# Five small edits to a hybrid attention and feed-forward block: the bias line by GpSimd copies, one transpose for the index weights, the values bank by bank, a split copy, and the last norm on VectorE

## The chip, the core and the metric

The program runs on one core of a Trainium2 chip. A core has a matrix engine (TensorE, PE in the profile, with its weight load PEld), VectorE (DVE), ScalarE (ACT), GpSimd (POOL) and SyncE (SP), which here issues most of the loads. The five run their own instruction streams and wait for each other on semaphores. DMAs are issued from SP, ScalarE or GpSimd. The metric is the device time of one execution in microseconds, the median over several runs; lower is better.

## The reference, cut to what matters

One layer on x of 512 frames by 1024 channels. All projections come from one matrix; branch A is sparse attention with an indexer that picks 128 keys for a query and a relative bias, branch B is stick-breaking attention. A gated MLP follows.

```python
q_a, k_a, v_a, q_i, k_i, w_i, q_s, k_s, v_s, g_a, g_b = split(x @ w_in)
w_i = w_i * 8 ** -0.5
# branch A, for a block of 128 queries
dots = einsum('thd,sd->ths', q_i, k_i) * 64 ** -0.5
score = einsum('th,ths->ts', w_i, relu(dots))      # chunk-causal
sel = top_k(score, 128)
logits = q_a @ k_a[sel] * 64 ** -0.5 + rel_bias[t5_bucket(sel - t)]
y_a = softmax(logits) @ v_a[sel]
# branch B
a = exp(log_sigmoid(z) + sum over later keys of log_sigmoid(-z));  y_s = a @ v_s
x = layer_norm(alpha * x + (sigmoid(g_a) * (y_a @ W_a) + sigmoid(g_b) * (y_s @ W_s)) @ w_out)
u, g = split(x @ w_ffn_in)
x = layer_norm(alpha * x + (gelu(causal_dwconv(u)) * g) @ w_ffn_out)
```

The bias depends on the distance alone. `t5_bucket` gives one of 32 buckets: distances 0 to 7 one each, then eight wider ones (from 8, 12, 16, 23, 32, 46, 64 and 91 on), and the same again for keys behind the query.

## The kernel before, in words

Every 32-bit operand of a matmul is split in a high part (rounded to the matrix engine's format) and the rest, so a product is three matmuls: high by high, high by low, low by high. For a weight piece, `Stream._advance` issues the load into one of three raw buffers (SP), the high copy on ScalarE (`whi_...`, L105) and the subtraction on VectorE or GpSimd (`wlo_...`, L107). A raw buffer can be loaded again once the subtraction has read it, so a piece three ahead is issued when that is done.

The program goes from stage to stage. Nine matmuls on zeros (`WARM`, into `idle_ps`) run while the first loads are on their way. Then come the indexer's queries (`qi0` to `qi7`, four PSUM banks `qi_ps`, 384 columns: the first 128 queries need no selection), the indexer's keys with the index weights (`ki`, 72 rows), and then a list of pieces, `FILL`: branch B's values `vs`, queries and keys `qs`, `ks`, the gates `gb`, branch A's `qa`, `ka`, `va`, with the heads of both branches worked in between. Values are made by `proj_v`: four weight pieces of two chunks each, four PSUM banks of one row block each, from the pool `psA` of four banks; `vs_ps` takes over the banks of `qi_ps`, so its matmuls into the fourth bank wait until the last indexer query (`qi3a`, `qi3b`, from `idx_queries`) has been read. When all is summed, ScalarE copies a bank's high part into `va`, VectorE writes the rest (L336, L337). `gb_ps` is the next user of the banks of `va_ps`.

The bias line holds, for each of 8 heads, the bias of all 640 distances. In before it is a product of a one-hot matrix (64x640, loaded by GpSimd in two halves) with the table's high and low parts (`rb`), in two matmuls (`line_ps`, L270), which ScalarE copies out negated (L271). GpSimd then stores it (`s_line`), and writes `s_win`, 128 shifted copies for every head, in DRAM. A head of branch A later loads its window `win` from there by SP (L483).

The index weights come out of the `ki` product as 8 rows and are needed as columns: three transposes of 8x128 into `wi_ps` (L367).

The order of all instructions is set by a scheduler with a timeline model, not written by hand, so an edit can move instructions in other places. The last part is the feed-forward product's last rows and the norm of the last row block (`finish(3)`), whose output goes out in three pieces.

Of the kernel before, what the change touches and what calls it, by code (L numbers as in the profile page):

```python
# [11 lines left out]
F32 = mybir.dt.float32  # L12
# [5 lines left out]
S = 512  # L18
D = 1024
DFF = 2816  # L20
H = 8
# [6 lines left out]
EPS = 1e-5  # L28
HT = 256
NSEL = 128  # L30
BIG = 1.0e30
INVALID = -3.0e38
TAKEN = -3.3e38
# [16 lines left out]
def r32(ap):  # L50
    return ap.bitcast(F32)


class Stream:


    def __init__(self, nc, raw, ring, pieces, ahead_load, ahead_split, place=None, lo_on_pool=()):
        self.nc, self.raw, self.ring, self.pieces = nc, raw, ring, pieces
        self.place = {} if place is None else place
        self.lo_on_pool = set(lo_on_pool)  # L60
        self.al, self.asp = ahead_load, ahead_split
        self.loaded, self.split, self.used = {}, {}, 0
        self.mixed, self.homes, self.direct, self.before = {}, {}, set(), {}
        self.nl = self.ns = 0

    def _advance(self, upto):
# [24 lines left out]
        while self.ns < min(n, upto + self.asp, self.nl):  # L91
            ts, w = self.loaded.pop(self.ns)
            key = self.pieces[self.ns][0]
            if key in self.direct:
                self.split[self.ns] = ts
                self.ns += 1
                continue
            if key in self.mixed:
                parts = self.mixed[key](ts)
            else:  # L100
                parts = [(ts[0], w, key)]
            out = ()
            for t, w, where in parts:
                hi, lo = self.tiles(where)
                nc.scalar.activation(hi[:, :w], t[:, :w], AF.Copy)  # L105
                eng = nc.gpsimd if key in self.lo_on_pool else nc.vector
                self.low = eng.tensor_sub(lo[:, :w], t[:, :w], r32(hi[:, :w])).ins  # L107
                out += (hi, lo)
            self.split[self.ns] = out
            self.ns += 1  # L110
# [20 lines left out]
def tile_block(ctx: ExitStack, tc: tile.TileContext, xT, xN, w_qi, w_ki, w_t, w_v, w_br, w_o, w_fi, w_fo,  # L131
# [10 lines left out]
    def padded(pool, shape, dt=F32, **kw):  # L142

        n = int(np.prod(shape[1:]))
        t = pool.tile([shape[0], -(-n // 32) * 32], dt, **kw)[:, :n]
        return t if len(shape) == 2 else t.rearrange("p (a b) -> p a b", a=shape[1])
# [84 lines left out]
    def load_x(key):  # L231
        k = int(key[2:])
        xraw[k] = bp.tile([128, 512], F32, tag="k", bufs=4, name=f"xr{k}")
        nc.sync.dma_start(xraw[k], xT[k * 128:(k + 1) * 128, :])

    for k in range(KC):
        st.before[f"qi{k}"] = load_x
    for k in range(KC):
# [15 lines left out]
    nc.gpsimd.dma_start(cwt.rearrange("p a b -> p (a b)"), cw)  # L254


    ohf = bp.tile([64, NREL], F32, tag="beta", bufs=2, name="ohf")
    oh = bp.tile([64, NREL], F32R, tag="beta", bufs=2, name="oh")
    rb = edge.tile([64, H], F32R, name="rb")
    rbf = padded(bp, [32, H], name="rbf")  # L260
    for r in (slice(0, 32), slice(32, 64)):
        nc.gpsimd.dma_start(ohf[r], onehot)
    nc.gpsimd.dma_start(rbf, rel)
    nc.gpsimd.tensor_copy(oh, ohf)
    nc.vector.tensor_copy(rb[0:32], rbf)
    nc.vector.tensor_sub(rb[32:64], rbf, r32(rb[0:32]))
    line = bp.tile([H, NREL], F32, tag="beta", bufs=2, name="line")
    for a, b in ((0, 512), (512, NREL)):
        ps = pb("line_ps")
        nc.tensor.matmul(ps[:H, :b - a], rb, oh[:, a:b], start=True, stop=True)  # L270
        nc.scalar.activation(line[:, a:b], ps[:H, :b - a], AF.Copy, scale=-1.0)  # L271
    s_line = nc.dram_tensor("s_line", (H, NREL), F32, kind="Internal").ap()
    s_win = nc.dram_tensor("s_win", (H, 128, 512), F32, kind="Internal").ap()
    nc.gpsimd.dma_start(s_line, line)
# [43 lines left out]
    def proj_v(which, name):  # L318

        pss = [pa(f"{name}_ps{i}") for i in range(NB)]  # L320
        for g in range(4):
            wh, wl = st.get(f"{which}{g}")
            for kk in range(2):
                k = 2 * g + kk
                c = slice(kk * 512, kk * 512 + 512)
                for i in range(NB):
                    r = slice(i * 128, i * 128 + 128)
                    nc.tensor.matmul(pss[i], xh[k][:, r], wh[:, c], start=(k == 0), stop=False)
                    nc.tensor.matmul(pss[i], xh[k][:, r], wl[:, c], start=False, stop=False)
                    nc.tensor.matmul(pss[i], xl[k][:, r], wh[:, c], start=False, stop=(k == KC - 1))  # L330
                    yield 3
        vt = []
        for i in range(NB):
            v = bp.tile([128, H, 2, 64], F32R, tag="v", bufs=4, name=f"{name}{i}")
            src = pss[i].rearrange("p (h d) -> p h d", h=H)
            nc.scalar.activation(v[:, :, 0, :], src, AF.Copy)  # L336
            nc.vector.tensor_sub(v[:, :, 1, :], src, r32(v[:, :, 0, :]))  # L337
            vt.append(v)
        return vt


# [2 lines left out]
    def idx_queries():  # L344
        for n in range(4):
# [6 lines left out]
            nc.vector.tensor_sub(b[0:64, late], ps[64:128], r32(b[64:128, late]))  # L352
            qi.extend((a, b))

    def idx_keys():
        ps = whole(proj_t("ki", M=72, bank=pb))
        kih = bp.tile([128, 512], F32R, tag="pt", bufs=8, name="kih")
        kil = bp.tile([128, 512], F32R, tag="pt", bufs=8, name="kil")
        wiT = bp.tile([8, 512], F32, tag="pt", bufs=8, name="wiT")
        nc.scalar.activation(wiT, ps[64:72], AF.Copy, scale=float(H) ** -0.5)  # L360
        for r in (slice(0, 64), slice(64, 128)):
            nc.scalar.activation(kih[r], ps[0:64], AF.Copy)
            nc.vector.tensor_sub(kil[r], ps[0:64], r32(kih[0:64]))
        wi = padded(cst, [128, 3, H], name="wi")
        ps = pb("wi_ps")
        for j in (1, 2, 3):
            nc.tensor.transpose(ps[:, (j - 1) * H:j * H], wiT[:, j * 128:j * 128 + 128], ident[:H, :H])  # L367
        nc.vector.tensor_copy(wi.rearrange("p a b -> p (a b)"), ps[:, :3 * H])
        index["k"] = kih, kil, wi

    score = {j: bp.tile([128, 128 * (j + 1)], F32, name=f"score{j}") for j in (1, 2, 3)}
# [539 lines left out]
    def finish(j):  # L911
        r = x1[j]
        mv, rstd = norm_stats(r, parts2[j])
        if j < 3:
            for c in (slice(0, 512), slice(512, 1024)):
                norm_apply(r, r, mv, rstd, g2, b2, c)
                nc.scalar.dma_start(out[j * 128:(j + 1) * 128, c], r[:, c])
            return
        cs = (slice(0, SHARE // 2), slice(SHARE // 2, SHARE), slice(SHARE, 1024))
        for c in (slice(512, 1024), slice(0, 512)):  # L920
            nc.vector.scalar_tensor_tensor(r[:, c], r[:, c], mv[:, 0:1], g2[:, c], op0=ALU.subtract, op1=ALU.mult)
        nc.scalar.activation(r[:, cs[2]], r[:, cs[2]], AF.Copy, scale=rstd)
        nc.gpsimd.tensor_add(r[:, cs[2]], r[:, cs[2]], b2[:, cs[2]])
        for c in cs[:2]:
            nc.vector.scalar_tensor_tensor(r[:, c], r[:, c], rstd, b2[:, c], op0=ALU.mult, op1=ALU.add)
        for c in cs:
            nc.scalar.dma_start(out[j * 128:(j + 1) * 128, c], r[:, c])


    for t in range(2):  # L930
# [123 lines left out]
```

## Time and profile before

| | us |
|---|---|
| median of 3 runs | 762.4 (762.27 to 762.73) |
| the profiled execution | 762.05 |
| its span, first to last instruction | 760.2 |
| TensorE busy | 751.1 (99%) |
| VectorE busy | 547.1 (72%) |
| ScalarE busy | 374.1 (49%) |
| GpSimd busy | 119.3 (16%) |
| moved by DMA | 107.09 MB, mean 141 GB/s |

A row of a timeline gives the start, the length, the engine, the line of the kernel, the operation, what it writes and reads, the form, a count of instructions in it, and in brackets the idle time in front of it with what ended it. A row of the waits gives who waited for what, the sum, how often and the longest. A row of the DMA issues gives what is loaded, the queue, the count, KB each, and the median from issue to landing. A matmul's length overlaps the next one's, so the distance between starts is what it costs.

### The profile page before, as it was taken

What the parts mean: (1) busy time and instruction counts of PE and PEld (TensorE: products, weight loads), DVE (VectorE), ACT (ScalarE), POOL (GpSimd) and SP (SyncE); (2) the same over time, 40 slices, a digit from 0 to 9 for tenths busy, and PEclk for the clock granted to TensorE, in tenths of its full rate; (3) what the DMA queues carried; (4) which work ended last, traced back from release to release, by engine and by line L of the source; (5) the groups of instructions that cost most, each with busy time, mean ns of one, the idle gap of its engine ahead of it and who ended that gap; (6) DMA issues with size and microseconds to landing.
All of it is one profiled execution on the core that took longest, in us unless ns stands there. A gap on an engine that the chain in (4) does not pass through costs nothing.

```text
span 760.2 us, 9908 instructions
## 1 busy us (share of the span) xinstructions
PE 751.1 (99%) x3597; PEld 630.3 (83%) x3597; DVE 547.1 (72%) x912; ACT 374.1 (49%) x601; POOL 119.3 (16%) x127
## 2 busy tenths in 40 slices
PE   9999999999999999999999999999999999999996
PEld 7788888888888888888889888888888888888885
DVE  6689587999675454458865778767877786777776
ACT  6554656555686857935311534433443443344320
POOL 3002555425834210000010000000000000000011
PEclk9999999999999999999999999999999999999999
DMA  8643423132333333126801554354434434445971
GB/s 258 225 155 100 123 83 111 57 111 84 111 98 97 102 106 99 55 78 203 328 1 42 166 181 147 117 180 170 135 138 164 169 129 147 168 153 157 340 291 56
DMA packets 38449, 107.09 MB, mean 141 GB/s; under 512 B 4536, under 2 KB 4936, under 8 KB 38400
## 3 DMA queue, kind: packets, MB, share of 16 engines
q1 hardware_dynamic: 34016, 95.73, 37.1%
q10 hardware_dynamic: 2576, 6.29, 3.2%
q0 software_dynamic: 1808, 4.44, 1.8%
q8 instruction: 28, 0.46, 0.2%
q14 instruction: 21, 0.17, 0.1%
HBM read 91.48 MB, written 12.87 MB: 137 GB/s over the span
## 4 chain that ended last, share of the span: by engine, by line
PE 92%; POOL 3%; issue 2%; DVE 2%; ACT 1%; DVEq 0%; POOLq 0%
PE u_ps L741 5%; PE u_ps L740 5%; PE g_ps L741 5%; PE u_ps L739 5%; PE g_ps L740 5%; PE g_ps L739 5%; PE m_ps L829 4%; PE m_ps L831 4%; PE m_ps L830 4%; PE av_ps L436 2%; PE ga_ps L285 2%; PE ga_ps L286 2%; PE ga_ps L287 2%; PE o_ps L698 2%; PE o_ps L699 2%
## 5 line engine op out<-in xcount | busy, mean ns | idle before, releaser
L739 PE MATMUL u_ps<-x1h,whi_u 128*128 128x512 f32 (+1 forms) x192 | 71.4, 372 | 0.0
L741 PE MATMUL u_ps<-x1h,wlo_u 128*128 128x512 f32 (+1 forms) x192 | 71.4, 372 | 0.0
L740 PE MATMUL u_ps<-x1l,whi_u 128*128 128x512 f32 (+1 forms) x192 | 71.3, 371 | 0.0
L739 PE MATMUL g_ps<-x1h,whi_g 128*128 128x512 f32 (+1 forms) x184 | 69.9, 380 | 0.0
L740 PE MATMUL g_ps<-x1l,whi_g 128*128 128x512 f32 (+1 forms) x184 | 69.9, 380 | 0.0
L741 PE MATMUL g_ps<-x1h,wlo_g 128*128 128x512 f32 (+1 forms) x184 | 69.9, 380 | 0.0
L748 POOL MEMSET u<- 128x2 f32 x22 | 2.1, 100 | 250.1 <-DVE c L753 250.1
L740 PEld LDWEIGHTS u_ps<-x1l,whi_u 128*128 128x128 f32 x192 | 36.2, 188 | 6.3
L739 PEld LDWEIGHTS u_ps<-x1h,whi_u 128*128 128x128 f32 x192 | 36.2, 188 | 6.2
L741 PEld LDWEIGHTS u_ps<-x1h,wlo_u 128*128 128x128 f32 x192 | 36.2, 188 | 6.2
L740 PEld LDWEIGHTS g_ps<-x1l,whi_g 128*128 128x128 f32 x184 | 34.6, 188 | 6.6
L739 PEld LDWEIGHTS g_ps<-x1h,whi_g 128*128 128x128 f32 x184 | 34.6, 188 | 6.5
L741 PEld LDWEIGHTS g_ps<-x1h,wlo_g 128*128 128x128 f32 x184 | 34.6, 188 | 6.5
L425 DVE TENSOR_TENSOR ptl<-tr_ps,pth 128x512 fp32r<-128x512 f32 (+1 forms) x48 | 27.4, 595 | 14.0 <-ACT pth L424 13.7
L107 DVE TENSOR_TENSOR wlo_u<-raw,whi_u 128x1024 fp32r<-128x1024 f32 x22 | 26.9, 1221 | 9.8 <-ACT whi_u L105 9.8
L105 ACT ACTIVATE whi_g<-raw 128x1024 fp32r<-128x1024 f32 x22 | 23.3, 1061 | 20.5 <-PE m_ps L831 13.6
L105 ACT ACTIVATE whi_pa<-raw 128x1024 fp32r<-128x1024 f32 x11 | 11.7, 1061 | 40.8 <-PE u_ps L740 32.3
L754 ACT ACTIVATE c<-c,cwt 128x512 f32<-128x512 f32 x22 | 15.8, 716 | 30.0 <-DVE c L753 30.0
L105 ACT ACTIVATE whi_u<-raw 128x1024 fp32r<-128x1024 f32 x22 | 23.3, 1060 | 13.9 <-PE u_ps L740 9.0
L107 DVE TENSOR_TENSOR wlo_g<-raw,whi_g 128x1024 fp32r<-128x1024 f32 x22 | 26.8, 1218 | 3.1 <-ACT whi_g L105 3.1
L488 POOL TENSOR_TENSOR bm<-win,score 128x256 f32<-128x256 f32 (+2 forms) x24 | 26.9, 1148 | 9.0 <-DVE mn L503 8.9
L758 DVE TENSOR_TENSOR hp<-g_ps,c 128x512 f32<-128x512 f32 x22 | 15.2, 691 | 17.3 <-PE g_ps L741 15.8
(559 smaller groups left out, 2205.9 us busy)
## 6 DMA issues: line engine op xcount, KB each, us to landing
raw<-in_w_fi_dram SPq DMA_DIRECT2D x44, 512.0 KB, 3.3
raw<-in_w_t_dram SPq DMA_DIRECT2D x32, 512.0 KB, 3.3
raw<-in_w_fo_dram SPq DMA_DIRECT2D x21, 512.0 KB, 3.5
rawb_p<-in_w_fo_dram SPq DMA_DIRECT2D x11, 512.0 KB, 3.7
d_z<-s_sum SPq DMA_DIRECT2D x10, 512.0 KB, 7.4
raw<-in_w_v_dram SPq DMA_DIRECT2D x8, 512.0 KB, 4.3
raw<-in_w_br_dram SPq DMA_DIRECT2D x8, 512.0 KB, 3.3
raw<-in_w_o_dram SPq DMA_DIRECT2D x8, 512.0 KB, 4.3
```

The costliest lines, as they stand in the source:

```text
L105: nc.scalar.activation(hi[:, :w], t[:, :w], AF.Copy)
L107: self.low = eng.tensor_sub(lo[:, :w], t[:, :w], r32(hi[:, :w])).ins
L285: nc.tensor.matmul(ps[:M], wh[:, c], xh[k], start=(k == 0), stop=False)
L425: lows = nc.vector.tensor_sub(tl[:, :width], ps[:, :width], r32(th[:, :width]))
L488: nc.gpsimd.tensor_add(bm[:, OFF[j]:OFF[j] + N], win[:, 512 - N:512], score[j])
L739: nc.tensor.matmul(ps[:, c], wh[:, kc], x1h[:, k, c], start=(k == 0), stop=False)
L740: nc.tensor.matmul(ps[:, c], wh[:, kc], x1l[:, k, c], start=False, stop=False)
L741: nc.tensor.matmul(ps[:, c], wl[:, kc], x1h[:, k, c], start=False, stop=(k == KC - 1))
L754: nc.scalar.activation(c, c, AF.Gelu_apprx_tanh, bias=cwt[:, f, 3:4])
L829: nc.tensor.matmul(o, xh_[:, r], wh[:, c], start=start, stop=False, skip_group_check=True)
L830: nc.tensor.matmul(o, xh_[:, r], wl[:, c], start=False, stop=False, skip_group_check=True)
L831: mm = nc.tensor.matmul(o, xl_[:, r], wh[:, c], start=False, stop=stop, skip_group_check=True)
```

## The change

Five edits. The bias line is written by GpSimd: the table is loaded turned (`relT`, 8x32), negated, and copied into the line in 18 pieces, one for each run of distances with one bucket. The one-hot matrix, `rb` and both matmuls go. The index weights are copied to rows 0, 32 and 64 of a zeroed 128x128 tile and transposed at once. In `proj_v`, the last of the four pieces is worked bank by bank, both chunks of a bank in a row, and each bank is copied out where its sum ends. The high copy of `qi0` is made in two halves. In the last norm VectorE does all three pieces itself, and the middle one goes out by SP instead of ScalarE.

```diff
+FAR = [8, 12, 16, 23, 32, 46, 64, 91]
...
-                nc.scalar.activation(hi[:, :w], t[:, :w], AF.Copy)
+                cuts = [0, w // 2, w] if key in self.halved else [0, w]
+                for a, b in zip(cuts, cuts[1:]):
+                    nc.scalar.activation(hi[:, a:b], t[:, a:b], AF.Copy)
...
+    st.halved.add("qi0")
...
-    ohf = bp.tile([64, NREL], F32, tag="beta", bufs=2, name="ohf")
-    oh = bp.tile([64, NREL], F32R, tag="beta", bufs=2, name="oh")
-    rb = edge.tile([64, H], F32R, name="rb")
-    rbf = padded(bp, [32, H], name="rbf")
-    for r in (slice(0, 32), slice(32, 64)):
-        nc.gpsimd.dma_start(ohf[r], onehot)
-    nc.gpsimd.dma_start(rbf, rel)
-    nc.gpsimd.tensor_copy(oh, ohf)
-    nc.vector.tensor_copy(rb[0:32], rbf)
-    nc.vector.tensor_sub(rb[32:64], rbf, r32(rb[0:32]))
+    relT = padded(bp, [H, 32], name="relT")
     line = bp.tile([H, NREL], F32, tag="beta", bufs=2, name="line")
-    for a, b in ((0, 512), (512, NREL)):
-        ps = pb("line_ps")
-        nc.tensor.matmul(ps[:H, :b - a], rb, oh[:, a:b], start=True, stop=True)
-        nc.scalar.activation(line[:, a:b], ps[:H, :b - a], AF.Copy, scale=-1.0)
+    nc.gpsimd.dma_start(relT, rel.rearrange("b h -> h b"))
+    nc.gpsimd.tensor_scalar(relT, relT, -1.0, None, op0=ALU.mult)
+    zero = S - 1
+    nc.gpsimd.tensor_copy(line[:, zero - 7:zero + 1], relT[:, 0:8][:, ::-1])
+    nc.gpsimd.tensor_copy(line[:, zero + 1:zero + 8], relT[:, 17:24])
+    for n, (lo_, hi_) in enumerate(zip(FAR, FAR[1:] + [S])):
+        for b, u0, u1 in ((8 + n, zero - hi_ + 1, zero - lo_ + 1), (24 + n, zero + lo_, min(zero + hi_, NREL))):
+            nc.gpsimd.tensor_copy(line[:, u0:u1], relT[:, b:b + 1].to_broadcast([H, u1 - u0]))
...
             wh, wl = st.get(f"{which}{g}")
-            for kk in range(2):
+            steps = [(kk, i) for kk in range(2) for i in range(NB)]
+            if g == 3:
+                steps.sort(key=lambda s_: s_[1])
+            for kk, i in steps:
...
+                if k == KC - 1:
+                    v = bp.tile([128, H, 2, 64], F32R, tag="v", bufs=4, name=f"{name}{i}")
+                    src = pss[i].rearrange("p (h d) -> p h d", h=H)
+                    nc.scalar.activation(v[:, :, 0, :], src, AF.Copy)
+                    nc.vector.tensor_sub(v[:, :, 1, :], src, r32(v[:, :, 0, :]))
+                    vt.append(v)
+                yield 3
...
-        nc.scalar.activation(wiT, ps[64:72], AF.Copy, scale=float(H) ** -0.5)
+        for j in (1, 2, 3):
+            nc.scalar.activation(wiT[32 * j - 32:32 * j - 24], ps[64:72, j * 128:j * 128 + 128], AF.Copy,
+                                 scale=float(H) ** -0.5)
...
-        for j in (1, 2, 3):
-            nc.tensor.transpose(ps[:, (j - 1) * H:j * H], wiT[:, j * 128:j * 128 + 128], ident[:H, :H])
-        nc.vector.tensor_copy(wi.rearrange("p a b -> p (a b)"), ps[:, :3 * H])
+        nc.tensor.transpose(ps[:, :128], wiT, ident)
+        nc.vector.tensor_copy(wi, ps[:, :96].rearrange("p (a b) -> p a b", b=32)[:, :, :H])
...
-        nc.scalar.activation(r[:, cs[2]], r[:, cs[2]], AF.Copy, scale=rstd)
-        nc.gpsimd.tensor_add(r[:, cs[2]], r[:, cs[2]], b2[:, cs[2]])
-        for c in cs[:2]:
+        for c, eng in zip(cs, (nc.scalar, nc.sync, nc.scalar)):
             nc.vector.scalar_tensor_tensor(r[:, c], r[:, c], rstd, b2[:, c], op0=ALU.mult, op1=ALU.add)
-        for c in cs:
-            nc.scalar.dma_start(out[j * 128:(j + 1) * 128, c], r[:, c])
+            eng.dma_start(out[j * 128:(j + 1) * 128, c], r[:, c])
```

What this does to the order of instructions is shown at three places. The rows name the line, the operation, what it writes and reads with the number of the buffer, the shape, and in brackets the semaphores it waits for (Pool, DVE, Activation and PE are engines, DMAHW the loads of SP and ScalarE, DMASW those of GpSimd).

GpSimd before the first head, before:

```order
L262 DMA ohf_323<-in_onehot_dram 32x640 x2
L263 DMA rbf_326<-in_rel_dram 32x8
L455 MEMSET keep_830 128x1
L215 AFFINE_SELECT first_96<-first_96 128x512 [waits Pool_49]
L455 MEMSET keep_931 128x1
L220 MEMSET mhalf_101 128x1 [waits Activation_49]
L264 CAST oh_324<-ohf_323 64x640 [waits DMASW2_49,DMASW3_49,DVE_49,PE_49]
L274 DMA s_line<-line_333 8x640 [waits Activation_49]
L275 DMA s_win<-s_line 1024x1x512 [waits DMASW5_49]
```

and after, from the scaling of the table on (its load stands behind that of cwt):

```order
L265 TENSOR_SCALAR relT_324<-relT_324 8x32 [waits DMASW2_49]
L267 COPY line_325<-relT_324 8x8 [waits Pool_49]
L268 COPY line_325<-relT_324 8x7
L271 COPY line_325<-relT_324 8x4 x4
L271 COPY line_325<-relT_324 8x7 x2
L271 COPY line_325<-relT_324 8x9 x2
L271 COPY line_325<-relT_324 8x14 x2
L271 COPY line_325<-relT_324 8x18 x2
L271 COPY line_325<-relT_324 8x27 x2
L271 COPY line_325<-relT_324 8x421
L271 COPY line_325<-relT_324 8x38
L274 DMA s_line<-line_325 8x640 [waits Pool_49]
```

The copies, which wait for GpSimd itself and the table's load (DMASW2), have taken the place of the CAST, and the store of the line no longer waits for ScalarE.

SP at the values' last pieces (w_v is vs0 to vs3 here, w_t the first piece of the list behind them, qs0), before:

```order
L87 DMA raw_11_0_369<-in_w_v_dram 128x1024 [waits DMAHW3_49,DMAHW0_49,DVE_49]
L87 DMA raw_12_0_418<-in_w_v_dram 128x1024 [waits DMAHW1_49,DVE_49]
L87 DMA raw_13_0_500<-in_w_t_dram 128x1024 [waits DMAHW5_49,DMAHW2_49,DVE_49]
L483 DMA win_1956<-s_win 128x512 [waits DMASW6_49]
L483 DMA win_2089<-s_win 128x512
L87 DMA raw_14_0_602<-in_w_t_dram 128x1024 [waits DMAHW3_49,DVE_49]
```

and after:

```order
L89 DMA raw_11_0_377<-in_w_v_dram 128x1024 [waits DMAHW3_49,DMAHW0_49,DVE_49]
L89 DMA raw_12_0_425<-in_w_v_dram 128x1024 [waits DMAHW1_49,DVE_49]
L488 DMA win_1963<-s_win 128x512 [waits DMAHW5_49,DMASW4_49]
L89 DMA raw_13_0_507<-in_w_t_dram 128x1024 [waits DMAHW2_49,DVE_49]
L488 DMA win_2096<-s_win 128x512
L89 DMA raw_14_0_609<-in_w_t_dram 128x1024 [waits DMAHW3_49,DVE_49]
```

The first of two window loads, which waits for `s_win` (DMASW), now stands ahead of the load of qs0.

TensorE and VectorE at the last piece of `va`. TensorE before (`va_ps0` to `va_ps3` are the four banks, `xh6` and `xh7` the two chunks):

```order
L328 MATMUL va_ps0_1940<-whi_va3_1946,xh6_283 128x512
L329 MATMUL va_ps0_1940<-wlo_va3_1947,xh6_283 128x512 [waits Pool_49]
L330 MATMUL va_ps0_1940<-whi_va3_1946,xl6_284 128x512
L328 MATMUL va_ps1_1941<-whi_va3_1946,xh6_283 128x512
L329 MATMUL va_ps1_1941<-wlo_va3_1947,xh6_283 128x512
L436 MATMUL av_ps_2052<-pth_2011,vs0_731 128x512 [waits DVE_49,Activation_49]
L330 MATMUL va_ps1_1941<-whi_va3_1946,xl6_284 128x512
L328 MATMUL va_ps2_1942<-whi_va3_1946,xh6_283 128x512
L436 MATMUL av_ps_2052<-ptl_2012,vs0_731 128x512 [waits DVE_49]
```

and after:

```order
L331 MATMUL va_ps0_1947<-whi_va3_1953,xh6_284 128x512
L332 MATMUL va_ps0_1947<-wlo_va3_1954,xh6_284 128x512 [waits Pool_49]
L333 MATMUL va_ps0_1947<-whi_va3_1953,xl6_285 128x512
L331 MATMUL va_ps0_1947<-whi_va3_1953,xh7_306 128x512
L332 MATMUL va_ps0_1947<-wlo_va3_1954,xh7_306 128x512
L441 MATMUL av_ps_2059<-pth_2018,vs0_720 128x512 [waits DVE_49,Activation_49]
L333 MATMUL va_ps0_1947<-whi_va3_1953,xl7_307 128x512
L331 MATMUL va_ps1_1948<-whi_va3_1953,xh6_284 128x512
L441 MATMUL av_ps_2059<-ptl_2019,vs0_720 128x512 [waits DVE_49]
```

The second chunk of the first bank (`xh7`, `xl7`) stood 17 rows behind the first one and now follows it at once. VectorE before:

```order
L503 ISA lg_2096,mn_2097<-l_ps_2100,bm_2092 128x512 [waits DMASW3_49,DMASW2_49,DMASW5_49,PE_49,Pool_49]
L503 ISA mn_2097 128x1
L503 ISA lg_2096,mn_2097<-l_ps_2105,win_2089 128x128 [waits PE_49]
L503 ISA mn_2097 128x1
L337 TENSOR_TENSOR va0_2201<-va_ps0_1940,va0_2201 128x8x64 [waits Activation_49]
L337 TENSOR_TENSOR va1_2204<-va_ps1_1941,va1_2204 128x8x64 [waits Activation_49]
```

and after:

```order
L508 ISA lg_2103,mn_2104<-l_ps_2107,bm_2099 128x512 [waits DMASW3_49,PE_49,Pool_49]
L508 ISA mn_2104 128x1
L338 TENSOR_TENSOR va0_2189<-va_ps0_1947,va0_2189 128x8x64 [waits Activation_49]
L508 ISA lg_2103,mn_2104<-l_ps_2112,win_2096 128x128 [waits PE_49]
L508 ISA mn_2104 128x1
L338 TENSOR_TENSOR va1_2199<-va_ps1_1948,va1_2199 128x8x64 [waits Activation_49]
```

The rest of the first bank (`va0`) is now taken ahead of the 128-column logits of branch A's head, and that of the second behind them.

Elsewhere a few matmuls of `qi` change places, and where the trace of before has 40 to 75 us some dots of the indexer move by a few matmuls against those of `vs`, `qs` and `ks`, and the copies of `vs` with them; the rest of the program stands in the same order.

More of the change, by code (lines that the diff above doesn't have):

```diff
@@ L63, in __init__ @@
         self.mixed, self.homes, self.direct, self.before = {}, {}, set(), {}
+        self.halved = set()
         self.nl = self.ns = 0
@@ L320, in proj_v @@
         pss = [pa(f"{name}_ps{i}") for i in range(NB)]
+        vt = []
         for g in range(4):
             wh, wl = st.get(f"{which}{g}")
-            for kk in range(2):
+            steps = [(kk, i) for kk in range(2) for i in range(NB)]
+            if g == 3:
+                steps.sort(key=lambda s_: s_[1])
+            for kk, i in steps:
                 k = 2 * g + kk
                 c = slice(kk * 512, kk * 512 + 512)
[L326 to L338, printed above, removed]
+                r = slice(i * 128, i * 128 + 128)
+                nc.tensor.matmul(pss[i], xh[k][:, r], wh[:, c], start=(k == 0), stop=False)
+                nc.tensor.matmul(pss[i], xh[k][:, r], wl[:, c], start=False, stop=False)
+                nc.tensor.matmul(pss[i], xl[k][:, r], wh[:, c], start=False, stop=(k == KC - 1))
+                if k == KC - 1:
[5 more added lines that the diff above has]
+                yield 3
         return vt
@@ L353, in idx_queries @@
             qi.extend((a, b))
+    wiT = bp.tile([128, 128], F32, name="wiT")
+    nc.gpsimd.memset(wiT, 0.0)
     def idx_keys():
@@ L358, in idx_keys @@
         kil = bp.tile([128, 512], F32R, tag="pt", bufs=8, name="kil")
-        wiT = bp.tile([8, 512], F32, tag="pt", bufs=8, name="wiT")
-        nc.scalar.activation(wiT, ps[64:72], AF.Copy, scale=float(H) ** -0.5)
+        for j in (1, 2, 3):
+            nc.scalar.activation(wiT[32 * j - 32:32 * j - 24], ps[64:72, j * 128:j * 128 + 128], AF.Copy,
+                                 scale=float(H) ** -0.5)
         for r in (slice(0, 64), slice(64, 128)):
```

## The prediction

> **What bounds the kernel now.** I read the busy shares first, then TensorE's waits over the whole run.
>
> ```profile
> PE 751.1 (99%) x3597; PEld 630.3 (83%) x3597; DVE 547.1 (72%) x912; ACT 374.1 (49%) x601; POOL 119.3 (16%) x127
> ...
> PE idle_ps L208 <- DVE idle L205: 1.2, 1, 1.2
> PE gb_ps L285 <- DVE va L337: 0.3, 1, 0.3
> ```
>
> TensorE (PE) is busy for 99% of the 760.2 us span and waits twice in all. An edit on another engine therefore pays only if it takes work off PE, closes that second wait, or shortens what stands after PE's last matmul. It costs only where it makes PE wait anew. The profiled execution took 762.05 us, 1.85 more than its span; the median of the runs is 762.4, so I work out a difference and put it on the median. About 0.2%, 1.5 us, is what a measurement of this kernel can tell from no change.
>
> **The bias line, on PE.** The timeline where its two matmuls stand (start, length):
>
> ```profile
> 15.44 0.86 PE L251 MATMUL qi_ps<-xh,wlo_qi 128*128 128x384 f32 x4
> 16.23 0.45 PE L270 MATMUL line_ps<-oh,rb 64*8 64x512 f32 x2
> 16.90 0.34 PE L250 MATMUL qi_ps<-xl,whi_qi 128*128 128x384 f32 x1
> ```
>
> Four matmuls of 384 columns take 0.86 and one alone 0.34, so they start (0.86 − 0.34)/3 = 0.173 apart. From 15.44 four of them and one more (L249) bring L250 to 16.31; it starts at 16.90. The line's matmuls thus cost 0.59. Without them everything behind could start 0.59 earlier, if what it needs is there.
>
> **Who is late next.** PE's first use of the fourth bank of vs_ps waits for VectorE's last indexer query (qi3b), which frees that bank:
>
> ```profile
> 16.72 8.50 SPq L87 DMA_DIRECT2D raw<-in_w_v_dram  x4
> 22.55 1.06 ACT L105 ACTIVATE whi_vs<-raw 128x1024 fp32r<-128x1024 f32 x1 [3.49 <-DMA raw<-in_w_v_dram]
> 23.64 1.22 DVE L107 TENSOR_TENSOR wlo_vs<-raw,whi_vs 128x1024 fp32r<-128x1024 f32 x1 [3.80 <-ACT whi_vs L105]
> 30.18 0.56 DVE L352 TENSOR_TENSOR qi3b<-qi_ps,qi3b 64x384 fp32r<-64x384 f32 x1
> 30.62 0.62 PE L328 MATMUL vs_ps<-whi_vs,xh 128*128 128x512 f32 x2
> ```
>
> The load of the first values weight (vs0) goes out at 16.72 and releases ScalarE at 22.55. From there VectorE works without a break (wlo_vs, the queries, wlo_vs, qi3a, qi3b) to 30.74. The second matmul of the last row, at 30.85 (0.62 less one matmul's 0.39 behind 30.62), is the one that needs the bank. Its margin is 0.11. If PE comes 0.59 earlier it stands there for about 0.48, since this chain hangs on the load and not on PE. Call d the shift of vs0's landing: the line part ends as d − 0.11, and never below −0.59.
>
> **What moves d.** The line is now written by 18 GpSimd copies behind a load of 256 four-byte numbers. What these stand against (GpSimd's timeline, its groups, and DMA issues with KB and us to landing):
>
> ```profile
> 9.79 0.80 POOL L264 CAST oh<-ohf 64x640 fp32r<-64x640 f32 x1 [4.53 <-DMA ohf<-in_onehot_dram]
> 18.25 0.54 POOL L274 DMA_DIRECT2D s_line<-line  x1 [7.66 <-ACT line L271]
> 23.99 1.13 POOL L275 DMA_DIRECT2D s_win<-s_line  x1 [5.20 <-DMA s_line<-line]
> ...
> L484 POOL MEMSET win<- 64x64 f32 x8 | 1.2, 146 | 54.1 <-DMA win<-s_win 54.1
> ...
> rbf<-in_rel_dram POOLq DMA_DIRECT2D x1, 1.0 KB, 6.0
> s_win<-s_line POOLq DMA_DIRECT2D x1, 2048.0 KB, 17.2
> raw<-in_w_t_dram SPq DMA_DIRECT2D x1, 512.0 KB, 6.9
> ...
> raw<-in_w_t_dram SPq DMA_DIRECT2D x32, 512.0 KB, 3.3
> ```
>
> GpSimd waited 4.53 for ohf, to 9.79. One load of 1 KB, which as rbf took 6.0, takes the place of three issues, so I put its landing near 9. One scaling and 18 copies cost 2.8 if each takes the 0.146 of a 64x64 memset, 15 if each takes the 0.80 of the CAST, and little over 0 if they overlap. I take 2.5, nearest the memset, since all but one copy write 8 rows of 38 numbers or fewer. The line is ready near 11.5 instead of 17.96. GpSimd was waiting in all of this (7.66 in the second row), so the copies hide. s_line and s_win follow as before, 5.74 apart: s_win is issued near 17.3 instead of 23.99, its traffic from about 18.9 on.
>
> [...]
>
> In before, s_win left at 23.99, when vs0 to vs2 had landed or nearly so. Now it meets them. Stretches by PE, PEld, DVE, ACT, POOL busy time, clock, DMA share, GB/s:
>
> ```profile
> 19.00:22.50 3.50, 3.50 (x22) 3.50 (x22) 0.76 (x1) 0.05 (x1) 0.00 (x0) 1.00 0.97 348
> 25.50:34.00 8.50, 8.50 (x38) 6.39 (x37) 7.61 (x11) 5.73 (x9) 0.00 (x0) 1.00 0.79 237
> ```
>
> From 19 to 22.5 the 16 engines are full without s_win. Beside s_win, from 25.5 to 34, all traffic together is 237 GB/s, and a 512 KB load takes 6.9 instead of the 3.3 of such loads later. So the upper end of d is +3.6. The lower end is −0.5: 160 KB of onehot (64x640 numbers of 4 bytes) are gone, at 348 GB/s 0.46 us of transfer ahead of the x and qi loads on which the issue at 16.72 hangs. Near which? vs0 is issued 2.2 before s_win's traffic begins, and at a landing of 3.3 to 5.8 most of its bytes are ahead of it; vs1 and vs2 behind it meet s_win fully, but ScalarE turns to vs1 only at 26.5. I take d = +0.4, nearer the lower end, so the line part is +0.3: the 0.59 that PE gains is lost, and a little more.
>
> The Trainium skill's "DMA: Bandwidth & Descriptors" (section "Issuing engines are not separate DMA queues") says that transfers issued by SP, ScalarE and GpSimd run on the same 16 engines and interleave, which speaks against the earlier s_win. The 6.9 against 3.3 agrees; it is the rule behind the slower rival below.
>
> On SP's queue one of the two win loads now stands ahead of the load of qs0 (raw_13 in the order).
>
> ```profile
> SPq L483 <- DMA s_win<-s_line: 11.2, 1, 11.2
> 41.24 1.06 ACT L105 ACTIVATE whi_qs<-raw 128x1024 fp32r<-128x1024 f32 x1 [1.52 <-PE vs_ps L330]
> ```
>
> That wait of 11.2 now holds qs0's load too. s_win should land near 17.3 + 17.2 = 34.5, plus up to 2 for sharing; the load then takes 3.3 to 6.9, so 38 to 43. ScalarE takes it at 41.24, after 1.52 of waiting for PE. I count 0; up to +1.5 if ScalarE's relus behind it run late and PE's dots with them. The next loads leave earlier than 42.08, since SP is free sooner.
>
> **Index weights.** Three transposes of eight rows become one of 128x128:
>
> ```profile
> 34.24 0.39 PE L329 MATMUL vs_ps<-wlo_vs,xh 128*128 128x512 f32 x1
> 34.56 0.35 PE L367 MATMUL wi_ps<-ident,wiT 8*128 8x8 f32 x3
> 34.84 0.50 PE L330 MATMUL vs_ps<-whi_vs,xl 128*128 128x512 f32 x1
> ...
> 206.49 0.49 PE L420 MATMUL tr_ps<-ident,lg 128*128 128x128 f32 x3
> 206.74 0.48 PE L330 MATMUL va_ps<-whi_va,xl 128*128 128x512 f32 x1
> ```
>
> A 512-column matmul holds PE 0.23 (0.62 less 0.39 above), so L330 could start at 34.47; with the transposes it starts some 0.48 later (its own length of 0.50 instead of 0.39 holds the last 0.11). Three 128x128 transposes take 0.25 at 206.49, 0.08 each. The part saves 0.40; bounds 0.2 and 0.48. ScalarE's three copies instead of one lie where PE waits for nothing, and cost nothing as long as they end before PE reaches 34.47; GpSimd's memset of wiT lies in the wait of 4.53.
>
> **Values' last piece.** ScalarE and VectorE at the wait that PE has left:
>
> ```profile
> 199.90 0.39 PE L330 MATMUL va_ps<-whi_va,xl 128*128 128x512 f32 x1
> 207.53 0.50 PE L285 MATMUL gb_ps<-xh,whi_gb 128*128 128x512 f32 x1 [0.32 <-DVE va L337]
> 202.23 0.37 ACT L424 ACTIVATE pth<-tr_ps 128x256 fp32r<-128x256 f32 x1
> 206.18 1.54 ACT L336 ACTIVATE va<-va_ps 128x512 fp32r<-128x512 f32 x3
> 204.35 0.68 DVE L503 CUSTOM_DVE_ANT_0 lg<-l_ps,bm 128x512 f32<-128x512 f32 x1
> 204.96 0.28 DVE L503 CUSTOM_DVE_ANT_0 lg<-l_ps,win 128x128 f32<-128x128 f32 x1
> 206.79 1.29 DVE L337 TENSOR_TENSOR va<-va_ps,va 128x512 fp32r<-128x512 f32 x2 [1.54 <-ACT va L336]
> 206.06 0.60 PE L499 MATMUL l_ps<-ka0b,qa0b 128*128 128x384 f32 x2
> ```
>
> Behind 206.74 and 0.23 for that matmul, gb_ps could start at 206.97; it starts at 207.53, 0.56 later. In the new order the first bank's last matmul stands where 199.90 stands now, ScalarE empties it behind the pth copy (from 202.6), VectorE right behind its 512-column lg (205.03) until 205.68 (half of 1.29), over 1 us before PE comes. Saved 0.56; bounds 0.32 (the wait as the profile labels it) and 0.56. That eviction now stands ahead of VectorE's 128-column lg, which moves from 205.24 to 205.96; l_ps of 384 columns waits for the bank that it frees, and starts at 206.06 plus two transposes put ahead of it, 206.23: 0.27 of margin. For vs PE waits nowhere in before; the dots around it move by a few rows, which I count at 0.
>
> **First weight's high half.** 0, since PE is in its nine warming matmuls until 5.22 and the half that is cut is done at 4.74; the cut's second start-up on ScalarE, some 0.1, can use the 0.48 up to there.
>
> ```profile
> 1.20 4.02 PE idle_ps L208 x9
> 4.11 0.63 ACT L105 ACTIVATE whi_qi<-raw 128x512 fp32r<-128x512 f32 x1
> ```
>
> **Last norm.**
>
> ```profile
> 752.85 0.41 DVE L907 SCALAR_TENSOR_TENSOR r<-m_end,r 128x256 f32<-128x256 f32 x1
> 755.61 1.61 DVE L925 SCALAR_TENSOR_TENSOR r<-r,rstd,ln 128x384 f32<-128x384 f32 x2
> ```
>
> The two 384s take 1.61 beside GpSimd's add, where 256 columns take 0.41, so that a 384 alone should take 0.62. Three in a row on VectorE are 0.41 + 0.62 + 0.62, to 757.26 instead of 757.22, less some overlap of one with the next. ScalarE issues two outputs instead of three, SP the other. I take −0.1; bounds −0.4 (the 1.61 less two of 0.62) and +0.1.
>
> **Sum.** +0.3 − 0.40 − 0.56 + 0 − 0.1 = −0.76: 761.3 for the profiled execution, 761.6 on the median.
>
> **Rivals.** (1) Nothing is late: onehot's absence brings vs0 0.5 earlier, and PE keeps its 0.59. Sum −0.59 − 0.40 − 0.56 − 0.1 = −1.65, 760.8; with the tail at its best 760.5. For it: s_win may start after vs0's bytes. Against: the full engines from 19 to 22.5. (2) Slower: the earlier s_win takes half of the engines from vs0's last bytes on, d = +3.6. Then +3.5 − 1.06 = +2.4, 764.8. It decides the sign from d = 1.2 on, and makes it measurably slower from d = 2.7 on. (3) The banks do not come free early, because ScalarE or VectorE reaches va later than I lay out: the 0.56 stays, and with d = 0.4 it is 762.2. (4) qs0's load behind the window holds PE by 1 to 1.5 on top of my sum: 762.6 to 763.1.
>
> **How the numbers follow.** Forecast with d between −0.3 and 1.2: 0.45. Rival 1: 0.25. Rival 2 with d over 1.2: 0.14, three fifths of it over 2.7. Rival 3: 0.07. Rival 4: 0.09. Faster by over 0.2% is under 760.9: rival 1's 0.25 and 0.04 of the forecast's lower edge, 0.29. Slower by over 0.2% is over 763.9: 0.08 of rival 2, 0.03 of the fourth with a larger d, and 0.03 for a stall in the reordered stretch from 40 to 75 that no row prices, 0.14. Between them 0.57. The range runs from rival 1 at its best, 760.5, to d = 2.2, 763.4, and leaves out most of rival 2.
>
> **What the profile after would show.** No line_ps on PE. s_win issued at 16 to 19. whi_vs starting within 0 to 1.2 of 22.55, and a new PE wait on VectorE's qi3b near 30 of 0.5 to 1. The wait of gb_ps gone. One transpose for wi_ps. The second win load early on SP and qs0's load behind it near 35. VectorE ending near 757 less the shift. If whi_vs starts by 22.1, rival 1 is right; past 24, rival 2.

## The result and the profile after

The changed kernel takes 772.27 us (median of 4 runs, 771.72 to 772.96), against 762.36 for the kernel before, measured beside it: ratio 1.013, 95% interval 1.0112 to 1.0147. The forecast was 761.6, with a range up to 763.4. The profiled execution took 771.72 us, its span 769.9; before, these were 762.05 and 760.2. So 9.7 us of span were added.

First the busy shares and TensorE's waits of the changed kernel, which answer to the first two views of before:

```profile
PE 761.3 (99%) x3593; PEld 628.8 (82%) x3593; DVE 547.7 (71%) x911; ACT 373.8 (49%) x601; POOL 123.7 (16%) x143
...
PE idle_ps L212 <- DVE idle L209: 1.2, 1, 1.2
```

PE has four instructions fewer, and the wait of `gb_ps` is gone, as it should be. Yet PE is busy for 10.2 us more. It isn't waiting longer; it is working more slowly. The granted clock doesn't explain it: the mean is 0.998 in both executions. The plainest sign is a stretch of 100 us in the feed-forward product, where neither the code nor its order was changed. First before, then after (columns: stretch, busy time of PE, PEld, DVE, ACT and POOL with counts, granted clock, DMA share, GB/s):

```profile
500.00:600.00 100.00, 100.00 (x443) 82.81 (x442) 74.82 (x110) 42.58 (x60) 0.80 (x8) 1.00 0.42 147
```

```profile
500.00:600.00 100.00, 100.00 (x432) 80.55 (x431) 71.45 (x105) 41.22 (x58) 0.70 (x7) 1.00 0.43 151
```

PE is full and at clock 1.00 in both, but has 432 matmuls in the 100 us instead of 443. The timeline shows the step from one to the next, before:

```profile
499.53 0.39 PE L741 MATMUL u_ps<-x1h,wlo_u 128*128 128x512 f32 x1
...
501.12 0.39 PE L739 MATMUL u_ps<-x1h,whi_u 128*128 128x512 f32 x1
```

and after:

```profile
500.09 0.39 PE L745 MATMUL g_ps<-x1l,whi_g 128*128 128x512 f32 x1
...
501.49 0.39 PE L745 MATMUL u_ps<-x1l,whi_u 128*128 128x512 f32 x1
```

There are seven steps between the two rows of before, 1.59/7 = 0.227 us each, and six between those of after, 1.40/6 = 0.233. Each 512-column matmul costs some 0.006 to 0.007 more, without a wait that a profile could list. By the start of the first `u_ps` the changed kernel is 2.76 late (408.79 against 406.03), by the last one 9.11 (691.56 against 682.45).

### The profile page after: what moved, and what is told of

Same layout as the page of the kernel before. It is cut to its first block, busy times and chain, and to the rows that moved or that the text cites. A ratio compares the mean times of both kernels' runs of the same rounds, so it can differ in the third digit from the quotient of the medians.

```text
span 769.9 us, 9907 instructions
## 1 busy us (share of the span) xinstructions
PE 761.3 (99%) x3593; PEld 628.8 (82%) x3593; DVE 547.7 (71%) x911; ACT 373.8 (49%) x601; POOL 123.7 (16%) x143
## 4 chain that ended last, share of the span: by engine, by line
PE 98%; DVE 1%; issue 0%; DVEq 0%
PE g_ps L746 5%; PE u_ps L746 5%; PE g_ps L745 5%; PE u_ps L745 5%; PE u_ps L744 5%; PE g_ps L744 5%; PE m_ps L834 4%; PE m_ps L835 4%; PE m_ps L836 4%; PE av_ps L441 3%; PE tr_ps L425 2%; PE gb_ps L287 2%; PE ga_ps L287 2%; PE ga_ps L286 2%; PE ga_ps L285 2%; PE gb_ps L286 2%
```

## The experiments

What the diff moves without showing it are addresses. A tile is a named buffer in the core's memory, and a pool a stretch of that memory for some tiles; pools are stacked from the left end or from the right one. `rb` (64 partitions of 8 numbers, 32 bytes in each) was the only tile of the small pool `edge`, which lies on the right-hand side of the core's memory, ahead of nearly all other tiles there. Without it, every tile on that side (`xh`, `xl`, `qi`, `r`, `x1h`, `x1l` and the rest) lies 32 bytes further on: `x1h` starts at byte 178880 of a partition before and at 178912 after, by the compiled program. The ring, the pool of the weights' high and low halves (`whi`, `wlo`) on the left, stays: the first `whi` is at 29888 in both. What a padding tile of so many bytes does can be tried without touching one instruction: in the kernels that only pad, every engine's instructions and order are those of the changed kernel. "Distance" below is that of right-hand tiles from the ring, counted from before's, which is 178880 − 29888 = 148992, 582 times 256. In the changed kernel it is +32.

**The 32 bytes given back.** The edit to the changed kernel:

```diff
+    pad = edge.tile([64, 8], F32, name="pad")
```

> The changed kernel with one unused tile of 32 bytes in the pool edge, where rb stood; every instruction stands in the same place as in the changed kernel. Theory A (layout): the removal of rb moved every tile on the right side by 32 bytes, from addresses that are a multiple of 64 to ones that are not, and each 512-column matmul on them takes 0.233 instead of 0.227. With the pad the spacing is 0.227 again and the time is the one that the five edits give alone, 760.0 to 761.6. Theory B (something else in the edits, such as the earlier traffic of s_win or the instruction stream, slows the matmuls): the pad changes nothing, 771.7 to 773.

It took 760.24 us (759.58 to 760.68) against 763.13 for before, measured beside it, ratio 0.9959 (0.9945 to 0.9973), span 758.5. The same stretch of it:

```profile
500.00:600.00 100.00, 100.00 (x443) 82.81 (x442) 76.28 (x112) 43.28 (x60) 0.79 (x8) 1.00 0.43 146
```

The 443 matmuls are back, and with them 11.4 us of span (769.9 to 758.5). This is the fast kernel, below. By the spans of the two traces the five edits themselves gain 1.7 us (760.2 to 758.5), and the shift of the tiles costs 11.4. The 1.7 is less sure than the 11.4: it hangs on one trace of each kernel, and by the medians the gain is 2.9 (760.24 against 763.13).

**The kernel before, pushed 32 bytes the other way.**

```diff
-    rb = edge.tile([64, H], F32R, name="rb")
+    rb = edge.tile([64, 2 * H], F32R, name="rb")[:, :H]
```

> The kernel before with rb 64 bytes wide instead of 32 (half of it unused), nothing else; every instruction stands in the same place. Theory A: all right-side tiles move by 32 bytes off the multiple of 64, the matmuls slow down as in the changed kernel, 771 to 774. Theory B: 762.4, as before.

774.03 us (773.85 to 775.91), ratio 1.0147 (1.0125 to 1.0168).

```profile
500.00:600.00 100.00, 100.00 (x432) 80.73 (x431) 71.55 (x105) 40.01 (x56) 0.70 (x7) 1.00 0.45 153
```

None of the five edits is in this kernel, and it is as slow as the changed one. The shift alone is enough.

**Padding of 96 bytes**, which puts the right-hand tiles at multiples of 128:

```diff
+    pad = edge.tile([64, 24], F32, name="pad")
```

> The changed kernel with an unused tile of 96 bytes in edge: right-side tiles at multiples of 128 bytes, where the kernel before has 64 beyond one. Theory A with a step of 64: the same as with 32 bytes of pad within 0.1%. Theory A with a step of 128: faster than it, by up to the same 7 ns for each matmul, some 10 us. Theory B: 771.7 to 773.

771.6 us (771.43 to 771.76), ratio 1.0108 (1.0092 to 1.0123). A start at a multiple of 128 doesn't help; the first theory, which asked for round addresses, fell here.

```profile
500.00:600.00 100.00, 100.00 (x432) 80.47 (x431) 71.47 (x105) 41.26 (x58) 0.70 (x7) 1.00 0.44 152
```

**Only the feed-forward tiles put back**, by padding where their pool opens:

```diff
+    pad = dp.tile([64, 8], F32, name="pad")
```

> The changed kernel with the unused 32 bytes in the pool dp, which opens after the attention part: the feed-forward part's tiles are back at multiples of 64, the attention part's are not. Theory A: the feed-forward matmuls are back at 0.227 and the 7.2 us that the changed kernel loses from 406 us on are gone, 764.6 to 765.6, with the attention part as slow as in the changed kernel (first u_ps near 408.8). Theory B: 771.7 to 773.

764.86 us (764.62 to 765.77), ratio 1.0023 (1.0014 to 1.0033), span 763.2. This shares out the 11.4: 763.2 − 758.5 = 4.7 belongs to the attention half, 769.9 − 763.2 = 6.7 to the feed-forward half. The two stretches of this kernel, one in each half:

```profile
110.00:150.00 40.00, 40.00 (x204) 33.62 (x203) 32.27 (x64) 23.84 (x44) 22.06 (x13) 1.00 0.27 84
500.00:600.00 100.00, 100.00 (x443) 82.81 (x442) 73.31 (x107) 42.45 (x59) 0.80 (x8) 1.00 0.45 153
```

In the fast kernel the first stretch holds 206 matmuls, but 2 in 200 is a thin difference (the changed kernel has 205). The start of the first `u_ps` shows it better, where the feed-forward half begins: 409.32 here, 408.79 in the changed kernel, 404.44 in the fast one.

**Address or distance?** Four kernels, measured beside each other, move one side or both. `shim` goes to the left side ahead of the ring, `pad` to the right.

```diff
 # all at multiples of 128: shim of 64 bytes, pad of 96
+    shim = cst.tile([64, 16], F32, name="shim")
+    pad = edge.tile([64, 24], F32, name="pad")
 # the ring at multiples of 128: shim of 64, pad of 32
+    shim = cst.tile([64, 16], F32, name="shim")
+    pad = edge.tile([64, 8], F32, name="pad")
 # the ring moved by 32, the right side as in the changed kernel
+    shim = cst.tile([64, 8], F32, name="shim")
 # pad of 160 alone
+    pad = edge.tile([64, 40], F32, name="pad")
```

> The changed kernel with 96 unused bytes in edge and 64 in the left-side pool cst: every tile, left (weights, raw buffers, heads) and right (xh, xl, x1h, x1l), lies at a multiple of 128 bytes. Same instructions in the same order. Theory A1 (a tile that streams through the matrix engine has to lie 64 bytes beyond a multiple of 128): slow as with 96 bytes of pad alone, and the products that stream a weight tile too, 772 to 777. Theory A2 (what counts is that the streamed tile and the tile held in the array lie alike modulo 128): as fast as with 32 bytes of pad, 759.5 to 761.

> The changed kernel with 32 unused bytes in edge (right side 64 beyond a multiple of 128, as in the kernel before) and 64 in cst (left side at multiples of 128). Theory A1: nearly as fast as with the right side alone put back, 760 to 766 (slower only where a weight streams). Theory A2: the two sides no longer match, 770 to 775.

> The changed kernel with its right side left as it is (96 beyond a multiple of 128) and the left side moved by 32 bytes to the same place. Theory A1: 772 to 777. Theory A2: 759.5 to 761; that would mend the changed kernel without touching a tile of the right side.

> The changed kernel with 160 unused bytes in edge: the right side 128 bytes further than with 32, so that both sides match modulo 128 but not modulo 256 or 512, which they do in the kernel before. A1 and A2 with a period of 128: 759.5 to 761. A2 with a period of 256 or 512: 770 to 774.

Before took 762.49 us beside them.

| kernel | distance, bytes against before | us | ratio (95%) |
|---|---|---|---|
| all at multiples of 128 | −128 | 771.51 | 1.0115 (1.01 to 1.013) |
| ring at multiples of 128 | −64 | 770.86 | 1.0107 (1.0092 to 1.0122) |
| ring moved by 32 | 0 | 760.37 | 0.9963 (0.9945 to 0.9982) |
| pad of 160 | −128 | 771.56 | 1.0117 (1.0102 to 1.0132) |

The third decides it:

```profile
500.00:600.00 100.00, 100.00 (x443) 82.81 (x442) 75.63 (x111) 43.05 (x60) 0.79 (x8) 1.00 0.43 145
```

Its right-hand tiles lie exactly where the slow kernel has them, and it is fast because the ring has moved along. So what counts is the distance and not the address, as far as one move of both sides by 32 bytes can tell. The first, with every tile at a multiple of 128, is slow; so a period of 128 is out.

**A period of 256 or of 512?** The right side moved back by a whole 256:

```diff
+    pad = edge.tile([64, 72], F32, name="pad")
```

> The changed kernel with 288 unused bytes in edge: the distance from the weight ring to x1h is 256 bytes less than in the kernel before, 128 less than with 160. Same instructions. If what counts is the distance modulo 256: fast, 759.5 to 761. If it is modulo 512 (the step from one 128-column block of a weight to the next is 512 bytes): slow, 770 to 774.

760.33 us (760.12 to 760.61) against 762.83 for before, ratio 0.9965 (0.9952 to 0.9978).

```profile
500.00:600.00 100.00, 100.00 (x443) 82.81 (x442) 75.48 (x111) 42.79 (x60) 0.80 (x8) 1.00 0.41 144
```

Fast at 0 and −256, slow at +32, −32, −64 and −128: what was tried fits a distance that is a multiple of 256 bytes.

**Which of the two reads is disturbed?** A feed-forward product of three matmuls reads the halves `x1h` and `x1l` as the 512 columns and `whi`, `wlo` as the held weights. Two kernels, made from the fast one, move one tile each by 32 bytes and give the rest of the 256 back behind it.

```diff
 # x1l alone: between x1h and x1l, and behind
+    qp.tile([128, 8], F32, name="shim_a")
     x1l = qp.tile([128, KC, S], F32R, name="x1l")
+    qp.tile([128, 56], F32, name="shim_b")
 # wlo alone: between the ring's whi and wlo buffers, and behind
...
+            self.ring.tile([128, 8], F32, tag="shim_a", bufs=1, name="shim_a")
...
+            self.ring.tile([128, 56], F32, tag="shim_b", bufs=1, name="shim_b")
...
```

> The changed kernel with 32 unused bytes in edge, and in the feed-forward part x1l alone moved by 32 bytes against the weight ring (x1h and all others stay alike modulo 256). Same instructions. If the pair of streamed tile and held weight decides, only the matmuls that stream x1l take 0.233 (a third of the part), those with x1h stay at 0.227, and the time is a third of 7.2 above it: 762.4 to 762.9 against 760.2. If the whole layout decides, all or none of them change: 760.2 or 767.

> The same, with the low halves of the weights (wlo) moved by 32 bytes in the ring, the high halves and all other tiles alike modulo 256. In the feed-forward part the order is whi with x1h, whi with x1l, wlo with x1h. Theory 'next': a matmul slows down when the weight that is loaded beside it, the next one, does not match the tile that it streams: then whi with x1l (ahead of wlo) takes 0.233 and wlo with x1h stays at 0.227. Theory 'held': the weight already in the array counts, so wlo with x1h takes 0.233 and whi with x1l stays. Either way about a third of the products, 763 to 764.5.

One run each, 765.38 and 772.29 us, beside 762.04 for before; neither time was expected. `wlo` moves for every weight, so the second kernel loses in the attention half too: its first `u_ps` starts at 408.87, against 404.82 in the first. Their feed-forward stretches, `x1l` first:

```profile
500.00:600.00 100.00, 100.00 (x434) 81.32 (x434) 72.55 (x106) 41.84 (x58) 0.80 (x8) 1.00 0.42 144
```

```profile
500.00:600.00 100.00, 100.00 (x431) 80.59 (x430) 71.55 (x105) 41.22 (x58) 0.69 (x7) 1.00 0.44 152
```

The mean step behind each of the three matmuls, worked out from their starts in the feed-forward part:

| kernel | `whi`·`x1h` | `whi`·`x1l` | `wlo`·`x1h` |
|---|---|---|---|
| fast | 0.2270 | 0.2268 | 0.2262 |
| changed | 0.2332 | 0.2336 | 0.2332 |
| `x1l` moved | 0.2315 | 0.2329 | 0.2307 |
| `wlo` moved | 0.2324 | 0.2386 | 0.2288 |

Neither the matmuls that use the moved tile, nor those beside which it is loaded, are slow alone: one odd tile slows all three, though not alike. With `wlo` moved the worst step is that of `x1l`, which stands ahead of a `wlo` matmul. That the two kinds of read disturb each other fits this, but it is not shown, and how they would do it stays open.

**The line part alone**, in the kernel before, with the 32 bytes kept:

```diff
-    rb = edge.tile([64, H], F32R, name="rb")
+    pad = edge.tile([64, 8], F32, name="pad")
+    relT = padded(bp, [H, 32], name="relT")
...
+    nc.gpsimd.tensor_copy(line[:, zero - 7:zero + 1], relT[:, 0:8][:, ::-1])
...
```

> The kernel before with the bias line by GpSimd copies as the only edit, and 32 unused bytes in edge in place of rb, so that no right-side tile moves. Theory (the line's matmuls cost TensorE 0.59 and nothing eats it, since the fourth bank of vs_ps has 2 us of margin): the end of the program 0.5 to 0.7 earlier by the trace, 761.8 or so on a median of 762.4. Rival (the prediction: the gain is lost to the wait for a bank): within 0.1, or up to 0.3 later. A part of it alone does not move the matmuls' spacing.

761.56 us, ratio 0.9981 (0.9972 to 0.9991). Its last `m_end` matmul starts 0.5 earlier than in before (751.87 against 752.37), so 0.5 of the line's 0.59 is kept.

**The values bank by bank, alone**, in the kernel before (the `proj_v` part of the diff):

```diff
-            for kk in range(2):
+            steps = [(kk, i) for kk in range(2) for i in range(NB)]
+            if g == 3:
+                steps.sort(key=lambda s_: s_[1])
+            for kk, i in steps:
...
```

> The kernel before with the values' last piece bank by bank as the only edit (the old line, rb in place). The scheduler moves some 200 matmuls between 30 and 210 us for it. Theory: the wait of gb_ps near 207 is gone and the end comes 0.5 to 0.6 earlier. Rival: a wait of the same size comes up elsewhere, the end within 0.2.

One run: 769.34 us, some 7 more than before, which neither theory had. The distance is that of before, and the stretch from 500 to 600 is at the fast pace (442 matmuls). The scheduler puts many matmuls elsewhere, and PE's longest wait is new. The wait, and two stretches around it:

```profile
PE va_ps L331 <- DVE ka1b L305: 2.8, 1, 2.8
...
187.00:192.00 5.00, 2.66 (x13) 1.86 (x11) 4.96 (x7) 1.66 (x2) 2.10 (x2) 1.00 0.30 105
192.00:200.00 8.00, 7.57 (x31) 6.33 (x32) 5.45 (x17) 3.71 (x9) 6.25 (x6) 0.79 0.10 33
```

PE is idle for nearly half of the first stretch, and in the second the granted clock is 0.79. The wait of 2.8 and the clock (0.21 of 8 us, 1.7) are 4.5 of the 7; the rest was not traced. The run says nothing on the price of this edit inside the changed kernel, whose order is another; it says that an edit can't be taken out of its company here.

**The window's store made early**, to see the collision that the forecast feared. From the fast kernel the 16 copies of the far distances are left out (the line is zeroed instead, so the bias of far distances is missing):

```diff
+    nc.gpsimd.memset(line, 0.0)
...
-    for n, (lo_, hi_) in enumerate(zip(FAR, FAR[1:] + [S])):
-        for b, u0, u1 in ((8 + n, zero - hi_ + 1, zero - lo_ + 1), (24 + n, zero + lo_, min(zero + hi_, NREL))):
-            nc.gpsimd.tensor_copy(line[:, u0:u1], relT[:, b:b + 1].to_broadcast([H, u1 - u0]))
```

> The changed kernel with 32 unused bytes in edge and without the 16 copies of the far distances (the line is filled with zero there, so the bias of those distances is left out). The copies took 0.42 each, 7.0 in all, so s_win leaves near 15.5 instead of 22.7, ahead of the first values weight (vs0). Theory 1 (s_win takes half of the DMA engines): whi_vs starts 1 to 3.6 later than 22.3; TensorE waits only from 3.5 of delay on (its first use is at 27.9 with 24.6 ready), so the end moves by less than 0.5. Theory 2 (it hides in the gaps of the queues): whi_vs within 0.5 of 22.3.

One run: 760.87 us, span 759.1. GpSimd's timeline, ScalarE's and the DMA issues of this kernel, and behind them what the fast kernel has for the same three:

```profile
14.15 1.13 POOL L274 DMA_DIRECT2D s_win<-s_line  x1 [2.81 <-DMA s_line<-line]
...
21.31 0.69 ACT L109 ACTIVATE whi_ki<-raw 128x576 fp32r<-128x576 f32 x1 [3.81 <-DMA raw<-in_w_ki_dram]
...
raw<-in_w_ki_dram SPq DMA_DIRECT2D x1, 288.0 KB, 6.1
```

```profile
22.66 1.13 POOL L276 DMA_DIRECT2D s_win<-s_line  x1 [4.85 <-DMA s_line<-line]
...
18.28 0.69 ACT L109 ACTIVATE whi_ki<-raw 128x576 fp32r<-128x576 f32 x1 [0.95 <-DMA raw<-in_w_ki_dram]
...
raw<-in_w_ki_dram SPq DMA_DIRECT2D x1, 288.0 KB, 3.0
```

The collision is real: beside `s_win` the index keys' load takes 6.1 us instead of 3.0, and ScalarE gets it 3.03 later. PE's last matmul moves by 0.2 (751.14 against 750.94). That 0.2 isn't the price of the collision in the forecast's order, though: without the copies the scheduler puts all indexer queries ahead of vs0's high copy on ScalarE, which starts at 25.92 instead of 22.31, and PE lists no wait for it. The experiment shows the contention and one order that absorbs it; what it would cost in the order of the changed kernel stays open.

## Why the prediction was wrong

**The step that failed** is the rule from which the sum was built: that an edit "costs only where it makes PE wait anew". So the sum had no term for where the tiles lie. It took each 512-column matmul outside the edits to cost what it cost before, 0.227 us, and the removal of `rb` was counted by the two matmuls that go with it. It also moved the tiles on one side by 32 bytes; each such matmul then took 0.233, worth +11.4 us (769.9 against 758.5, same instructions in the same order), with no new wait. No rival named it; the slower one, 764.8 by a collision of loads, is not what happened. In the changed kernel `s_win` left at 21.28, not at 17.3, and vs0 was taken earlier than the 22.55 of before:

```profile
21.28 1.13 POOL L275 DMA_DIRECT2D s_win<-s_line  x1 [4.57 <-DMA s_line<-line]
22.20 1.06 ACT L109 ACTIVATE whi_vs<-raw 128x1024 fp32r<-128x1024 f32 x1 [3.46 <-DMA raw<-in_w_v_dram]
```

**The rest of the sum can be read in the fast kernel**, whose span is 758.5 against before's 760.2, −1.7. That is close to the first rival (−1.65) and not to the forecast (−0.76). The medians lie further off still: the three kernels at a distance of 0 and −256 are 2.1 to 2.9 below before (760.37 against 762.49, 760.33 against 762.83, 760.24 against 763.13). The terms below are read from the two traces alone.

The line part, forecast +0.3, kept its gain. It failed twice. First, d: vs0's landing was put 0.4 late, and came 0.24 early (22.55 in before).

```profile
22.31 1.06 ACT L109 ACTIVATE whi_vs<-raw 128x1024 fp32r<-128x1024 f32 x1 [3.34 <-DMA raw<-in_w_v_dram]
9.90 7.02 POOL L272 COPY line<-relT 8x4 f32<-8x4 f32 x16
```

The copies were priced at 2.5 us from a memset; the 16 of the second row alone (of all widths; the row gives the form of the first) take 7.02, 0.44 each. So `s_win` left at 22.66, not at 17.3, after vs0 had landed, and there was no collision. That was luck: the copies hide behind GpSimd's wait as the forecast said, but what kept `s_win` off vs0 is that they were nearly three times as slow as it had them. Second, the margin: the row at 30.62 was read as PE's first use of the fourth bank. It is of the third, which is free from 28.33 on, when VectorE's qi2b ends; the fourth is first written by the second matmul of the other row here, both of before:

```profile
27.77 0.56 DVE L352 TENSOR_TENSOR qi2b<-qi_ps,qi2b 64x384 fp32r<-64x384 f32 x1
...
32.66 0.62 PE L328 MATMUL vs_ps<-whi_vs,xh 128*128 128x512 f32 x2
```

That is 32.89 against 30.74 for qi3b: 2.1 of margin, not 0.11. By these rows vs0 could have come 1.5 late without taking back the 0.59, and the wait on qi3b that the forecast looked for is listed neither for the changed nor for the fast kernel. The rows leave out buffer numbers, and the forecast gave a row to a bank without counting. The last `qi_ps` matmul starts 0.65 earlier (22.17 against 22.82), and no wait takes it back. With the line part alone the end came 0.5 earlier, so some of the 0.65 belongs to other edits or to chance.

The index weights, forecast −0.40, are worth −0.36. In the fast kernel:

```profile
33.82 0.39 PE L334 MATMUL vs_ps<-whi_vs,xl 128*128 128x512 f32 x1
34.06 0.27 PE L373 MATMUL wi_ps<-ident,wiT 128*128 128x128 f32 x1
...
34.40 0.40 PE L333 MATMUL vs_ps<-wlo_vs,xh 128*128 128x512 f32 x1
```

From 33.82 to 34.40 are two matmuls and the transpose, 0.58; before, the same took 0.94 (34.24 to 35.18).

The values' last piece, forecast −0.56, came as said: the wait is gone, and PE's lead over before grows from 1.03 at the last `va_ps` to 1.51 at the first `gb_ps` and 1.59 at `bs_ps`.

```profile
205.71 0.47 PE L334 MATMUL va_ps<-whi_va,xl 128*128 128x512 f32 x1
206.02 0.40 PE L286 MATMUL gb_ps<-xh,whi_gb 128*128 128x512 f32 x1
```

The split copy, forecast 0: PE's first `qi_ps` matmul starts at 4.57 instead of 4.79 (4.66 in the changed kernel), but the fast kernel then lists a wait of 0.2 on `whi_qi`, and the lead isn't seen apart in what follows. `qs0`'s load behind the window held nothing: PE has no wait there.

The last norm, forecast −0.1, gave about −0.3. From the last `m_end` matmul's start to the end of the span it takes 758.5 − 750.94 = 7.56 us instead of 760.2 − 752.37 = 7.83.

```profile
754.00 1.53 DVE L929 SCALAR_TENSOR_TENSOR r<-r,rstd,ln 128x256 f32<-128x256 f32 x3
```

Three pieces on VectorE alone take 1.53, less than the two beside GpSimd's add (1.61). The term was mis-sized, inside its bounds of −0.4 and +0.1. Together: −0.65 − 0.36 − 0.56 − 0.3, less the 0.16 by which the lead shrinks from 1.59 to 1.43 between `bs_ps` and the last `m_end`, is the −1.7.

## What to carry to other kernels

Removing or adding a tile moves others: before an edit is timed, compare the addresses of the tiles that the hot matmuls read, and if they moved, pad them back first, so that the edit and the layout are measured apart. Where PE is full, without waits, at the same clock, and still has fewer matmuls in the same 100 us, compare the step between starts: that is where such a loss shows, and in no list of waits. The best version here is the changed kernel with 32 unused bytes, 760.24 us against 763.13 for before.

## What the runs showed of the hardware that I had not expected

A 512-column fp32 matmul of this kernel starts every 0.227 us if the streamed and the held tiles lie a multiple of 256 bytes apart, and some 0.233 if they lie 32, 64 or 128 off (443 against 432 in 100 us); moving both by 32 bytes together changed nothing, and one odd tile among four gave 0.229 to 0.239. That PE's own reads are what collides is the nearest reading and was only argued; other sizes, types and offsets below 32 were not tried. GpSimd's copies of 8 rows (4 to 421 numbers wide, most under 40) cost 0.44 us on the mean in the fast kernel and 0.40 in the changed one (6.37 for the 16), some three times its 64x64 memset (0.146). Width doesn't set their time: the four of 8x4 took 0.176 each in the fast kernel and 0.570 on the mean in the one with the pad of 288, the two of 8x27 0.737 and 0.198. Why is open. After a wait of 2.8 us, the one kernel that had one ran a stretch of 8 us at a mean granted clock of 0.79.
